# Forgetting attention with the values as TensorE's loaded operand, and its output normalised by channels

## The chip, the core and the metric

The kernel is one program on one NeuronCore of a Trainium2 chip. The core has five engines that run at the same time, each with its own list of instructions, which it works through in the order in which it stands: TensorE (PE in the profile) multiplies matrices, VectorE (DVE) and ScalarE (ACT) work on tiles elementwise, GpSimd (POOL) does so in software, and SyncE (SP) issues most of the transfers. An engine waits at an instruction until what the instruction reads has been written and the buffer that it writes is free; what stands behind it in the list waits too. The metric is the device time of one execution in microseconds (us).

## The reference, cut to what matters

Two layers work on a sequence of 256 tokens with 2048 channels. Each layer has three token mixers side by side, an output projection, and a feed-forward network. The change is in the first mixer, attention with a forget gate ("fox"): 8 heads of 64 channels.

```python
c = jnp.cumsum(jax.nn.log_sigmoid(f_logit + f_bias), axis=1)
for i in range(S // 128):                       # two blocks of 128 queries
    s = einsum('bhqd,bhkd->bhqk', q[q0:end], k[:end]) * scale
    s = s + c[q0:end, None] - c[None, :end]
    p = softmax(where(mask, s, -inf), axis=-1)
    outs.append(einsum('bhqk,bhkd->bhqd', p, v[:end]))
...
fox = rmsnorm(fox, fox_out_norm[l])             # over the 512 channels of a token
mix = concatenate([fox, gla, lru], axis=-1) @ w_out[l]
x = x + mix
```

## The kernel before, in words

Every large product is made of float32 numbers that are split in two parts, high and low. A weight block is loaded (`raw`), ScalarE casts it to the high part `wh`, VectorE subtracts to get the low part `wl`, and TensorE adds three products (hi by `wh`, hi by `wl`, lo by `wh`). The left side of a product is held transposed, channels on partitions, also as hi and lo.

The output projection is two such products, `op` 0 and 1, each of 1024 output columns and 16 steps k of 128 channels. One step is 12 matmuls of 512 columns: two token blocks, two column halves, three products. `wh` and `wl` have four buffers each, so ScalarE and VectorE can be at most four steps ahead of TensorE. The steps go through the mixers' outputs in the order `mt[2]`, `mt[3]` (the recurrent branch), `mt[1]` (gated linear attention), `mt[0]` (fox): fox's channels are steps 12 to 15 of 16, and the last two steps run after a regrouping (lines L207 to L209 instead of L216 to L219).

The softmax of fox is woven into the first of the two products: the generator `softmax` is resumed once a step. Its work goes by units: unit 0 and 1 hold four heads each of the first query block (h = 0, 128 keys), units 2 to 5 two heads each of the second (h = 1, 256 keys). They are taken in three pairs. For a pair TensorE makes the scores (`fs`), VectorE adds the gate bias and takes the row maximum, ScalarE takes the exponential and sums it by rows (`pt`, `sums`), TensorE transposes the weights (`pp`, line L938) and ScalarE copies them out (`pT`). `attend(h)` then multiplies: `pT` is loaded into the array (128 keys by 128 queries) and 64 channels of values are streamed, so that the output `fo` has queries on partitions. It is divided by the sums (L953), squared and summed (L957), and multiplied by 1/sqrt(mean square), which GpSimd computes as a power of -0.5 of one number per partition (`rstd_of`, L172). At the end `split_T` transposes the result (`tp`, L181), multiplies by the gain and writes hi and lo into `mt[0]`. The other norms of the kernel use `rstd_of` too, with one to four numbers per partition.

The program is written in the order of the data; a scheduler then sets the order of each engine's list from priorities (casts and subtractions of weights come first) and from its own estimate of durations. The small PSUM tiles (`auxt`) share two buffers.

Of the kernel before, what the change touches and what calls it, by code (L numbers as in the profile page):

```python
# [9 lines left out]
F32 = mybir.dt.float32  # L10
# [6 lines left out]
P = 128  # L17
L = 2
S = 256
NH = 2  # L20
# [28 lines left out]
def trunk(ctx, tc, x, xcols, w_in, w_out, w_gate, w_up, w_down, vecs, w2, wblk, gfin, consts, masks, out):  # L49
# [66 lines left out]
        nc.sync.dma_start(mflat, masks.rearrange("p a b -> p (a b)"))  # L116
        V.tensor_copy(msk.rearrange("p a b -> p (a b)"), mflat)

    mhalf = cp.tile([P, 8], F32, name="mhalf")
    V.memset(mhalf, -0.5)  # L120

    ls4 = cp.tile([P, L, NCT], F32, name="ls4")
# [356 lines left out]
    def mixers(l, xt, steps, mp):  # L479
# [413 lines left out]
            with tc.high_priority(SOONEST):  # L893
                V.tensor_tensor(fk[:, i], fk[:, i], bx, op=ALU.mult)
        rest(steps)
        sums = mp.tile([P, NH, 8], F32, name="sums", tag="sums")
        pTs, ons = {}, []
        units = [(h, [2 * b + e for b in range(b0, b0 + 4 // (h + 1))])
                 for h in range(NH) for b0 in range(0, 4, 4 // (h + 1)) for e in range(2)]

# [10 lines left out]
        def weights_of(n, sp):  # L911
            h, hds = units[n]
            nk, per = P * (h + 1), len(hds)
            pt = mp.tile([P, per, nk], F32, name="pt", tag=("gqk0", "gqk1", "la")[n % 3])
            mx = sm.tile([P, 4], F32, name="mx", tag="mx")
            for i, hd in enumerate(hds):
                if h == 0:
                    V.tensor_tensor_reduce(pt[:, i, :], sp[:, i * nk:(i + 1) * nk], nb00[:, hd, :], 1.0, -3.0e38,
                                           ALU.subtract, ALU.max, mx[:, i:i + 1])
                else:  # L920
                    for kb in range(2):
                        sl = slice(kb * P, (kb + 1) * P)
                        V.tensor_tensor_reduce(pt[:, i, sl], sp[:, i * nk + kb * P:i * nk + (kb + 1) * P], ck[kb][:, hd, :], 1.0,
                                               -3.0e38, ALU.subtract, ALU.max, mx[:, 2 * kb + i:2 * kb + i + 1])
# [1 line left out]
                V.tensor_tensor(mx[:, 0:2], mx[:, 0:2], mx[:, 2:4], op=ALU.max)  # L926
            V.tensor_scalar(mx[:, :per], mx[:, :per], -1.0, None, op0=ALU.mult)
            for i, hd in enumerate(hds):
                A.activation(pt[:, i, :], pt[:, i, :], AF.Exp, bias=mx[:, i:i + 1], accum_out=sums[:, h, hd:hd + 1])
            return pt  # L930

        def flip(n, pt):
# [8 lines left out]
            for i, hd in enumerate(hds):  # L941
                pTs[h, hd] = pT[:, i, :]

        def attend(h):
            o = auxt("fo")
            for hd in range(FOX_H):
                sl = slice(hd * 64, (hd + 1) * 64)
                for kb in range(h + 1):
                    T.matmul(o[:, sl], pTs[h, hd][:, kb * P:(kb + 1) * P], fv[kb][:, sl], start=kb == 0, stop=kb == h)
            rs = sm.tile([P, 8], F32, name="rs", tag="rs")  # L950
            V.reciprocal(rs, sums[:, h, :])
            on = mp.tile([P, FOX_W], F32, name="on", tag="gz", bufs=2)
            V.tensor_tensor(on.rearrange("p (h d) -> p h d", d=64), o.rearrange("p (h d) -> p h d", d=64),  # L953
                            rs.unsqueeze(2).to_broadcast([P, 8, 64]), op=ALU.mult)
            fss = sm.tile([P, 1], F32, name="fss", tag="fss")
            jk = mp.tile([P, FOX_W], F32, name="jk", tag="b1")
            A.activation(jk, on, AF.Square, accum_out=fss)  # L957
            rf = rstd_of(fss, FOX_W, 1, f"rf{l}{h}")
            V.tensor_scalar(on, on, rf, None, op0=ALU.mult)
            ons.append(on)  # L960

        mt[0] = mp.tile([P, 2, 4, S], F32R, name="mt0", tag="tok")

        def softmax():
            for n in range(0, len(units), 2):
                pts = pair(n)
                yield
                if n == 2:
                    attend(0)
                yield  # L970
                for e in range(2):
                    flip(n + e, pts[e])
                yield
            attend(1)
            yield
            for j in (0, 2):
                yield
                split_T(lambda h, i: ons[h][:, i * P:(i + 1) * P], lambda i: vc(V_FOXN + i), mt[0], j, 2)


        order = [2, 3, 1, 0]
# [89 lines left out]
```

## Time and profile before

| what | us |
|---|---|
| median of three runs | 2075.72 |
| lowest and highest run | 2075.49, 3631.46 |
| the profiled execution | 2075.76 |
| its span, first to last instruction | 2074.0 |

The profiled execution is one of those whose time agrees with the median; the 3631.46 us run is not what the profile shows. Between the span and the execution's time lie 1.8 us. A view of the profile names an engine, a source line, the operation, and the tiles it writes and reads (out<-in). A float32 matmul stands there as two rows, so that the 8 matmuls of `attend(0)` are 16 rows. TensorE's rows overlap: a matmul's own duration is longer than the distance to the next one, and it is the distance that counts.

### The profile page before, as it was taken

What the parts mean: (1) busy time and instruction counts of PE and PEld (TensorE: products, weight loads), DVE (VectorE), ACT (ScalarE), POOL (GpSimd) and SP (SyncE); (2) the same over time, 40 slices, a digit from 0 to 9 for tenths busy, and PEclk for the clock granted to TensorE, in tenths of its full rate; (3) what the DMA queues carried; (4) which work ended last, traced back from release to release, by engine and by line L of the source; (5) the groups of instructions that cost most, each with busy time, mean ns of one, the idle gap of its engine ahead of it and who ended that gap; (6) DMA issues with size and microseconds to landing.
All of it is one profiled execution on the core that took longest, in us unless ns stands there. A gap on an engine that the chain in (4) does not pass through costs nothing.

```text
span 2074.0 us, 30220 instructions
## 1 busy us (share of the span) xinstructions
PE 2058.0 (99%) x11918; PEld 1860.4 (90%) x11918; DVE 1333.5 (64%) x1730; ACT 1109.1 (53%) x1557; POOL 15.6 (1%) x26
## 2 busy tenths in 40 slices
PE   9999999999999999999999999999999999999998
PEld 7899888999998899998899998899999888999987
DVE  7787755666655556655578878666666555665654
ACT  6875555545543445554468655555555444455543
POOL 0000000000000000000000000000000000000000
PEclk9999999999999999999999999999999999999999
DMA  8566545666666666666655665456666666666664
GB/s 320 159 195 194 186 160 186 200 203 203 204 203 200 206 203 200 198 199 202 198 193 173 187 217 163 161 191 203 203 203 199 198 204 206 199 199 200 201 203 163
DMA packets 302878, 408.76 MB, mean 197 GB/s; under 512 B 11744, under 2 KB 196624, under 8 KB 302608
## 3 DMA queue, kind: packets, MB, share of 16 engines
q1 hardware_dynamic: 298112, 403.14, 59.9%
q10 hardware_dynamic: 4624, 3.70, 0.6%
q8 instruction: 93, 1.52, 0.3%
q14 instruction: 49, 0.40, 0.1%
HBM read 404.68 MB, written 2.11 MB: 196 GB/s over the span
## 4 chain that ended last, share of the span: by engine, by line
PE 96%; issue 2%; DVE 1%; ACT 0%; POOL 0%; ACTq 0%; POOLq 0%
PE gu L263 30%; PE gu L264 15%; PE dn L219 6%; PE dn L217 6%; PE dn L216 6%; PE lg L263 2%; PE op L216 2%; PE op L219 2%; PE op L217 2%; PE lx L263 2%; PE dn L208 1%; PE dn L209 1%; PE dn L207 1%; PE gqk L263 1%; PE fq L263 1%
## 5 line engine op out<-in xcount | busy, mean ns | idle before, releaser
L263 PE MATMUL gu<-x,wh 128*128 128x512 f32 x2816 | 914.4, 382 | 0.0
L289 DVE TENSOR_TENSOR wl<-raw,wh 128x1024 fp32r<-128x1024 f32 (+1 forms) x465 | 567.1, 1222 | 375.0 <-ACT wh L288 375.0
L264 PE MATMUL gu<-x,wl 128*128 128x256 f32 x2816 | 739.3, 273 | 0.0
L288 ACT CAST wh<-raw 128x1024 fp32r<-128x1024 f32 (+1 forms) x465 | 487.0, 1050 | 450.9 <-PE gu L263 361.2
L263 PEld LDWEIGHTS gu<-x,wh 128*128 128x128 f32 x2816 | 519.7, 189 | 64.7
L264 PEld LDWEIGHTS gu<-x,wl 128*128 128x128 f32 x2816 | 539.9, 192 | 9.3
L234 DVE TENSOR_TENSOR wl<-raw,wh 128x1024 fp32r<-128x1024 f32 (+2 forms) x288 | 351.5, 1226 | 268.1 <-ACT wh L233 267.6
L233 ACT CAST wh<-raw 128x1024 fp32r<-128x1024 f32 (+2 forms) x288 | 299.8, 1047 | 340.2 <-PE dn L219 191.5
L216 PE MATMUL dn<-wh,ht 128*128 128x512 f32 x568 | 215.6, 380 | 0.0
L217 PE MATMUL dn<-wl,ht 128*128 128x512 f32 x568 | 215.3, 379 | 0.0
L219 PE MATMUL dn<-wh,ht 128*128 128x512 f32 x568 | 169.0, 379 | 0.0
L219 PEld LDWEIGHTS dn<-wh,ht 128*128 128x128 f32 x568 | 107.4, 189 | 15.2
L217 PEld LDWEIGHTS dn<-wl,ht 128*128 128x128 f32 x568 | 107.4, 189 | 15.1
L216 PEld LDWEIGHTS dn<-wh,ht 128*128 128x128 f32 x568 | 107.4, 189 | 15.2
L314 ACT COPY half<-gu 128x256 f32<-128x256 f32 x176 | 64.9, 369 | 46.6 <-PE gu L263 40.9
L263 PE MATMUL lg<-xt,wh 128*128 128x512 f32 x256 | 86.5, 392 | 0.7 <-DVE lg L315 0.7
L263 PE MATMUL lx<-xt,wh 128*128 128x512 f32 x256 | 84.2, 388 | 2.1 <-ACT wh L288 1.9
L216 PE MATMUL op<-wh,mt 128*128 128x512 f32 x192 | 74.8, 390 | 0.0
L217 PE MATMUL op<-wl,mt 128*128 128x512 f32 x192 | 73.8, 384 | 0.0
L264 PE MATMUL lg<-xt,wl 128*128 128x256 f32 x256 | 67.2, 273 | 0.0
L264 PE MATMUL lx<-xt,wl 128*128 128x256 f32 x256 | 65.0, 275 | 0.4 <-DVE wl L289 0.2
L219 PE MATMUL op<-wh,mt 128*128 128x512 f32 x192 | 58.2, 382 | 0.0
(304 smaller groups left out, 2449.6 us busy)
## 6 DMA issues: line engine op xcount, KB each, us to landing
raw<-in_w_gate SPq DMA_DIRECT2D x176, 512.0 KB, 3.5
raw<-in_w_up SPq DMA_DIRECT2D x176, 512.0 KB, 4.5
raw<-in_w_down SPq DMA_DIRECT2D x176, 512.0 KB, 4.3
raw<-in_w_in SPq DMA_DIRECT2D x55, 1024.0 KB, 5.1
raw<-in_w_out SPq DMA_DIRECT2D x64, 512.0 KB, 4.4
raw<-in_w_in SPq DMA_DIRECT2D x17, 512.0 KB, 3.7
raw<-in_w_in SPq DMA_DIRECT2D x16, 528.0 KB, 3.7
raw<-in_w_in SPq DMA_DIRECT2D x16, 520.0 KB, 3.7
```

The lines of the kernel that those rows point to most:

```text
L207: T.matmul(out, hi, turns(wh[:, cols[i]]), start=k == 0, stop=False)
L208: T.matmul(out, hi, turns(wl[:, cols[i]]), start=False, stop=False)
L216: T.matmul(out, hi, turns(wh[:, c]), start=k == 0, stop=False)
L217: T.matmul(out, hi, turns(wl[:, c]), start=False, stop=False)
L219: T.matmul(inturn(ps[i][h][:, :segs[i][1]]), lo, turns(wh[:, c]), start=False, stop=k == nk - 1)
L233: A.copy(wh, raw[:, j:j + jn, :tot])
L234: V.tensor_tensor(wl, raw[:, j:j + jn, :tot], f(wh), op=ALU.subtract)
L263: both = lambda: T.matmul(ps[i].rearrange("p (a t u) -> p a t u", a=2, u=2), wh[:, c], turns(xk), start=k == 0, stop=k == KT - 1)
L264: low = lambda: T.matmul(inturn(ps[i][:, 0:S]), wl[:, c], turns(xk[:, 0]), start=False, stop=False)
L288: A.copy(wh[:, js], raw[:, rs, :])
L289: V.tensor_tensor(wl[:, js], raw[:, rs, :], f(wh[:, js]), op=ALU.subtract)
L314: mark(A.copy(two(c), halves_of(ps[:, S:])))
```

## The change

`weights_of` keeps the row sums of a unit (`sm4`), takes their reciprocal on VectorE and multiplies the whole weight tile `pt` (128x512) by it, before the transposes. `attend` loads 64 channels of the values and streams the 128 queries of `pT`; the output has channels on partitions, an even head in partitions 0 to 63 and an odd one in 64 to 127. ScalarE copies it to `on` and squares it; VectorE adds the four channel groups of the squares in two steps. A new function `norm` adds over partitions with a matmul against ones, which leaves the sum of squares of a query in every partition, and computes the power of -0.5 of the 128x128 tile on GpSimd; `mhalf` is made 128 wide for that. The gain, the factor and the split into hi and lo follow. The 16 transposes of `on` over both layers go away. `softmax` calls `norm(0)` one pair later than `attend(0)`, and `norm(1)` one step after `attend(1)`.

```diff
-    mhalf = cp.tile([P, 8], F32, name="mhalf")
+    mhalf = cp.tile([P, P], F32, name="mhalf")
...
             for i, hd in enumerate(hds):
-                A.activation(pt[:, i, :], pt[:, i, :], AF.Exp, bias=mx[:, i:i + 1], accum_out=sums[:, h, hd:hd + 1])
+                A.activation(pt[:, i, :], pt[:, i, :], AF.Exp, bias=mx[:, i:i + 1], accum_out=sm4[:, i:i + 1])
+            V.reciprocal(sm4[:, :per], sm4[:, :per])
+            V.tensor_tensor(pt, pt, sm4[:, :per].unsqueeze(2).to_broadcast([P, per, nk]), op=ALU.mult)
...
         def attend(h):
             o = auxt("fo")
-            for hd in range(FOX_H):
-                sl = slice(hd * 64, (hd + 1) * 64)
+            for b in range(FOX_H // 2):
                 for kb in range(h + 1):
-                    T.matmul(o[:, sl], pTs[h, hd][:, kb * P:(kb + 1) * P], fv[kb][:, sl], start=kb == 0, stop=kb == h)
-            rs = sm.tile([P, 8], F32, name="rs", tag="rs")
-            V.reciprocal(rs, sums[:, h, :])
...
-            A.activation(jk, on, AF.Square, accum_out=fss)
-            rf = rstd_of(fss, FOX_W, 1, f"rf{l}{h}")
-            V.tensor_scalar(on, on, rf, None, op0=ALU.mult)
+                    for e in range(2):
+                        hd = 2 * b + e
+                        T.matmul(o[e * 64:(e + 1) * 64, b * P:(b + 1) * P], fv[kb][:, hd * 64:(hd + 1) * 64],
+                                 pTs[h, hd][:, kb * P:(kb + 1) * P], start=kb == 0, stop=kb == h)
+            on = mp.tile([P, 4, P], F32, name="on", tag="gz", bufs=2)
+            A.copy(on, o.rearrange("p (b q) -> p b q", b=4))
+            jk = mp.tile([P, 4, P], F32, name="jk", tag="b1")
+            A.activation(jk, on, AF.Square)
+            for w in (2, 1):
+                V.tensor_tensor(jk[:, 0:w], jk[:, 0:w], jk[:, w:2 * w], op=ALU.add)
+            return on, jk
+        def norm(h, on, jk):
+            sq = auxt("bc")
+            T.matmul(sq[:, 0:P], ones, jk[:, 0], start=True, stop=True)
+            m, r = (mp.tile([P, P], F32, name=n, tag=n) for n in ("rfm", "rfr"))
+            V.tensor_scalar(m, sq[:, 0:P], 1.0 / FOX_W, EPS, op0=ALU.mult, op1=ALU.add)
+            G.tensor_tensor(r, m, mhalf, op=ALU.pow)
+            V.tensor_tensor(on, on, vec[:, l, V_FOXN:V_FOXN + 4].unsqueeze(2).to_broadcast([P, 4, P]), op=ALU.mult)
+            V.tensor_tensor(on, on, r.unsqueeze(1).to_broadcast([P, 4, P]), op=ALU.mult)
+            hi, lo = (mt[0][:, i, :, h * P:(h + 1) * P] for i in range(2))
+            A.copy(hi, on)
+            V.tensor_tensor(lo, on, f(hi), op=ALU.subtract)
...
-            for j in (0, 2):
-                yield
-                split_T(lambda h, i: ons[h][:, i * P:(i + 1) * P], lambda i: vc(V_FOXN + i), mt[0], j, 2)
+            last = attend(1)
+            yield
+            norm(1, *last)
+            yield
```

In the changed kernel's line numbers, L906 is the scores, L940 the transposes `pp`, L955 `fo`, L968 the matmul against ones (its output tile is called `bc`), L970 and L971 the mean square and the power, L972 and L973 the gain and the factor, L975 and L976 hi and lo.

Where the instructions stand is shown at the two norms of the first layer; the second layer's lists are the same there. First VectorE's list of the kernel before, around the norm of query block 0; `rf` is GpSimd's power of one column, `wl` (L234) are low weight parts:

```order
L953 TENSOR_TENSOR on<-fo,rs 128x512 [waits PE_49]
L926 TENSOR_TENSOR mx<-mx 128x2 [waits DVE_49]
L927 TENSOR_SCALAR mx<-mx 128x2 [waits DVE_49]
L170 TENSOR_SCALAR rf00m<-fss 128x1 [waits Activation_49]
L959 TENSOR_SCALAR on<-on,rf_2787 128x512 [waits Pool_49]
L234 TENSOR_TENSOR wl<-raw,wh 128x1024 [waits DMAHW5_49,DMAHW4_49,Activation_49]
```

The same place in the changed kernel; the first `wl` here is step 10 of the first product, the first `pt` is unit 4, the second unit 5:

```order
L970 TENSOR_SCALAR rfm<-bc 128x128 [waits PE_49]
L930 RECIPROCAL sm_2852<-sm_2852 128x2 [waits Activation_49]
L931 TENSOR_TENSOR pt<-pt,sm_2852 128x512 [waits DVE_49]
L973 TENSOR_TENSOR on<-on,rfr 128x512 [waits Pool_49]
L234 TENSOR_TENSOR wl<-raw,wh 128x1024 [waits DMAHW7_49,DMAHW6_49,Activation_49]
L930 RECIPROCAL sm_2865<-sm_2865 128x2 [waits Activation_49]
L976 TENSOR_TENSOR mt_2617<-on,mt_2617 128x4x128 [waits Activation_49]
L931 TENSOR_TENSOR pt<-pt,sm_2865 128x512 [waits DVE_49]
L234 TENSOR_TENSOR wl<-raw,wh 128x1024 [waits Activation_49]
```

Before, the wait for GpSimd stands ahead of one multiplication and the weights' low parts; now it also stands ahead of the multiplication of unit 5's softmax weights.

TensorE's list of the changed kernel, from the last row of step 7 on; the `bc` of query block 0, the matmul against ones, stands 12 matmuls earlier, ahead of step 7. The first four `pp` are unit 4, the last row is unit 5's first:

```order
L219 MATMUL op_0_1_1_2663<-wh,mt_109 128x512
L940 MATMUL pp<-cst,pt 128x128 [waits DVE_49,PE_49,Activation_49]
L940 MATMUL pp<-cst,pt 128x128
L940 MATMUL pp<-cst,pt 128x128 [waits Activation_49]
L940 MATMUL pp<-cst,pt 128x128
L216 MATMUL op_0_0_0_2660<-wh,mt_2401 128x512
L217 MATMUL op_0_0_0_2660<-wl,mt_2401 128x512
L216 MATMUL op_0_1_0_2662<-wh,mt_2401 128x512
L217 MATMUL op_0_1_0_2662<-wl,mt_2401 128x512
L219 MATMUL op_0_0_0_2660<-wh,mt_2401 128x512
L940 MATMUL pp<-cst,pt 128x128 [waits DVE_49,Activation_49]
```

The same transposes in TensorE's list before, between steps 7 and 8:

```order
L219 MATMUL op_0_1_1_2658<-wh,mt_109 128x512
L938 MATMUL pp<-cst,pt 128x128 [waits PE_49,Activation_49]
L938 MATMUL pp<-cst,pt 128x128
L938 MATMUL pp<-cst,pt 128x128 [waits Activation_49]
L938 MATMUL pp<-cst,pt 128x128
L938 MATMUL pp<-cst,pt 128x128 [waits PE_49,Activation_49]
```

They waited for ScalarE's exponentials; now they wait for VectorE as well, and unit 5's have moved five matmuls into step 8.

The norm of query block 1, in VectorE's list before:

```order
L953 TENSOR_TENSOR on<-fo,rs 128x512 [waits DVE_49,PE_49]
L170 TENSOR_SCALAR rf01m<-fss 128x1 [waits Activation_49]
L959 TENSOR_SCALAR on<-on,rf_2959 128x512 [waits Pool_49]
L234 TENSOR_TENSOR wl<-raw,wh 128x1024 [waits Activation_49]
L234 TENSOR_TENSOR wl<-raw,wh 128x1024 [waits DMAHW3_49,DMAHW2_49,Activation_49]
```

and in the changed kernel, where the one `wl` between L973 and L976 is step 13:

```order
L962 TENSOR_TENSOR jk<-jk 128x256 [waits Activation_49]
L972 TENSOR_TENSOR on<-on,vec 128x512
L962 TENSOR_TENSOR jk<-jk 128x128 [waits DVE_49]
L970 TENSOR_SCALAR rfm<-bc 128x128 [waits PE_49]
L973 TENSOR_TENSOR on<-on,rfr 128x512 [waits Pool_49]
L234 TENSOR_TENSOR wl<-raw,wh 128x1024 [waits Activation_49]
L976 TENSOR_TENSOR mt_2617<-on,mt_2617 128x4x128 [waits Activation_49]
```

TensorE's list of the changed kernel has the second `bc` after step 9, then steps 10 and 11, and then step 12, the first that reads fox's `mt[0]` (here `mt_2617`); its first six matmuls are of query block 0, the others of block 1:

```order
L219 MATMUL op_0_0_0_2660<-wh,mt_2617 128x512
L219 MATMUL op_0_1_0_2662<-wh,mt_2617 128x512
L216 MATMUL op_0_0_1_2661<-wh,mt_2617 128x512 [waits Activation_49]
L217 MATMUL op_0_0_1_2661<-wl,mt_2617 128x512
L216 MATMUL op_0_1_1_2663<-wh,mt_2617 128x512
L217 MATMUL op_0_1_1_2663<-wl,mt_2617 128x512
L219 MATMUL op_0_0_1_2661<-wh,mt_2617 128x512 [waits DVE_49]
```

In the kernel before, two groups of four transposes `tp` stood there, one after step 10 and one after step 11; now nothing but the steps stands between the second `bc` and the wait.

## Rows read from the trace of the kernel before

**Rows 1.** The page: busy time, share of span, instructions; chain that ended last, by engine.

```profile
PE 2058.0 (99%) x11918; PEld 1860.4 (90%) x11918; DVE 1333.5 (64%) x1730; ACT 1109.1 (53%) x1557; POOL 15.6 (1%) x26
...
PE 96%; issue 2%; DVE 1%; ACT 0%; POOL 0%; ACTq 0%; POOLq 0%
```

**Rows 2.** TensorE's waits in the whole span: total us, times, longest.

```profile
PE lx L263 <- ACT wh L288: 1.9, 2, 1.4
```

**Rows 3.** Windows of the first layer's softmax stretch: busy us of each engine, clock, DMA.

```profile
255.00:265.00 10.00, 10.00 (x58) 7.67 (x57) 6.68 (x25) 7.77 (x25) 0.00 (x0) 1.00 0.34 107
265.00:275.00 10.00, 10.00 (x54) 8.16 (x54) 6.03 (x27) 5.82 (x14) 0.55 (x1) 1.00 0.41 125
```

**Rows 4.** GpSimd's groups by shape: busy us, mean ns of one, idle before.

```profile
L717 POOL MEMSET kt<- 128x512 f32 x4 | 2.0, 524 | 689.4 <-PE dn L209 689.1 <-POOLq L1060 0.3
L702 POOL MEMSET gqm<- 128x1024 f32 x2 | 1.9, 960 | 147.0 <-DVE ti L565 147.0
L172 POOL TENSOR_TENSOR r<-r400m,mhalf 128x4 f32<-128x4 f32 x1 | 1.0, 1008 | 44.8 <-DVE r400m L170 44.8
...
L172 POOL TENSOR_TENSOR r<-r21m,mhalf 128x2 f32<-128x2 f32 x1 | 0.7, 701 | 63.4 <-DVE r21m L170 63.4
...
L172 POOL TENSOR_TENSOR rf<-rf00m,mhalf 128x1 f32<-128x1 f32 x1 | 0.5, 547 | 42.4 <-DVE rf00m L170 42.4
```

**Rows 5.** Timeline of the first norm: start, duration, engine, line, idle before and releaser.

```profile
266.56 0.55 POOL L172 TENSOR_TENSOR rf<-rf00m,mhalf 128x1 f32<-128x1 f32 x1 [42.43 <-DVE rf00m L170]
267.15 0.49 DVE L959 TENSOR_SCALAR on<-on,rf 128x512 f32<-128x512 f32 x1 [0.66 <-POOL rf L172]
```

**Rows 6.** VectorE's groups by shape, 245 to 303 us.

```profile
L234 DVE TENSOR_TENSOR wl<-raw,wh 128x1024 fp32r<-128x1024 f32 x16 | 19.5, 1224 | 13.2 <-ACT wh L233 12.9
...
L953 DVE TENSOR_TENSOR on<-fo,rs 128x512 f32<-128x512 f32 x2 | 1.4, 690 | 1.2 <-PE fo L949 1.2
...
L951 DVE RECIPROCAL rs<-sums 128x8 f32<-128x8 f32 x2 | 0.4, 198 | 0.0
...
L170 DVE TENSOR_SCALAR rf00m<-fss 128x1 f32<-128x1 f32 x1 | 0.2, 154 | 0.5 <-ACT jk L957 0.5
```

**Rows 7.** ScalarE's groups by shape, 245 to 303 us.

```profile
L940 ACT COPY pT<-pp 128x512 f32<-128x512 f32 x6 | 3.3, 574 | 0.1
...
L957 ACT ACTIVATE jk<-on 128x512 f32<-128x512 f32 x2 | 1.3, 634 | 4.3 <-DVE on L953 4.3
```

**Rows 8.** TensorE's timeline, first layer's output projection.

```profile
250.60 1.88 PE L907 MATMUL fs<-fk,fq 64*128 64x128 f32 x16 [0.73 <-DVE mt L186]
252.42 0.48 PE L209 MATMUL op<-wh,mt 128*128 128x512 f32 x1
...
276.48 1.09 PE L938 MATMUL pp<-cst,pt 128*128 128x128 f32 x8
277.32 0.46 PE L216 MATMUL op<-wh,mt 128*128 128x512 f32 x1
...
279.99 3.68 PE L949 MATMUL fo<-fv,pT 128*128 128x64 f32 x32
283.48 0.46 PE L216 MATMUL op<-wh,mt 128*128 128x512 f32 x1
...
286.15 0.38 PE L216 MATMUL op<-wh,mt 128*128 128x512 f32 x1
...
288.74 0.60 PE L181 MATMUL tp<-cst,on 128*128 128x128 f32 x4
289.10 0.46 PE L216 MATMUL op<-wh,mt 128*128 128x512 f32 x1
```

**Rows 9.** Windows at the end of the span: columns as in rows 3.

```profile
2064.00:2066.00 2.00, 1.36 (x7) 0.85 (x5) 1.72 (x3) 0.95 (x3) 0.00 (x0) 1.00 0.85 314
...
2068.00:2070.00 2.00, 0.00 (x0) 0.00 (x0) 0.88 (x2) 1.33 (x2) 0.03 (x1) 0.50 0.28 109
```

**Rows 10.** TensorE's timeline at the start of the span.

```profile
1.19 4.45 PE L104 MATMUL wp<-warm 128*128 128x512 bf16 x10 [1.19 <-DVE xp L523]
```

More of the change, by code (lines that the diff above doesn't have):

```diff
@@ L895, in mixers @@
         rest(steps)
-        sums = mp.tile([P, NH, 8], F32, name="sums", tag="sums")
-        pTs, ons = {}, []
+        pTs = {}
         units = [(h, [2 * b + e for b in range(b0, b0 + 4 // (h + 1))])
@@ L915, in weights_of @@
             mx = sm.tile([P, 4], F32, name="mx", tag="mx")
+            sm4 = sm.tile([P, 4], F32, name="sm4", tag="sm4")
             for i, hd in enumerate(hds):
@@ L942, in flip @@
                 pTs[h, hd] = pT[:, i, :]
+        mt[0] = mp.tile([P, 2, 4, S], F32R, name="mt0", tag="tok")
         def attend(h):
             o = auxt("fo")
-            for hd in range(FOX_H):
-                sl = slice(hd * 64, (hd + 1) * 64)
+            for b in range(FOX_H // 2):
                 for kb in range(h + 1):
-                    T.matmul(o[:, sl], pTs[h, hd][:, kb * P:(kb + 1) * P], fv[kb][:, sl], start=kb == 0, stop=kb == h)
-            rs = sm.tile([P, 8], F32, name="rs", tag="rs")
@@ L951, in attend @@
-            V.reciprocal(rs, sums[:, h, :])
[L952 to L956, printed above, removed]
-            A.activation(jk, on, AF.Square, accum_out=fss)
-            rf = rstd_of(fss, FOX_W, 1, f"rf{l}{h}")
@@ L959, in attend @@
-            V.tensor_scalar(on, on, rf, None, op0=ALU.mult)
-            ons.append(on)
-        mt[0] = mp.tile([P, 2, 4, S], F32R, name="mt0", tag="tok")
+                    for e in range(2):
[3 more added lines that the diff above has]
+            on = mp.tile([P, 4, P], F32, name="on", tag="gz", bufs=2)
@@ L964, in softmax @@
         def softmax():
+            last = None
             for n in range(0, len(units), 2):
@@ L968, in softmax @@
                 if n == 2:
-                    attend(0)
+                    last = attend(0)
+                elif n == 4:
+                    norm(0, *last)
                 yield
@@ L973, in softmax @@
                 yield
-            attend(1)
+            last = attend(1)
             yield
-            for j in (0, 2):
-                yield
-                split_T(lambda h, i: ons[h][:, i * P:(i + 1) * P], lambda i: vc(V_FOXN + i), mt[0], j, 2)
+            norm(1, *last)
+            yield
         order = [2, 3, 1, 0]
```

## The prediction

> **What bounds the kernel now.** I read the page's busy times first, then the chain of work that ended last, then TensorE's waits. TensorE is busy 99% of the span and makes up 96% of the chain [rows 1], and its longest sum of waits for one thing is 1.9 us [rows 2]. So every microsecond that is added to or taken from TensorE's list counts, and so does every wait that the change puts into it, while work on the other engines costs something only where TensorE comes to wait for it. Then I read the windows of the stretch that the change touches: in the softmax stretch of the first layer TensorE has no idle time at all, VectorE is busy 6.0 to 6.7 us in 10 and ScalarE 5.8 to 7.8 [rows 3]. There is room for some more work there, but each of these engines goes through its list in order, so what matters is where in the list a long wait stands.
>
> **The power on GpSimd.** This is the term that decides. Before, GpSimd raises one, two or four numbers per partition: 547 ns, 701 ns and 1008 ns [rows 4]. One more column costs 154 ns, two more 307 ns, so the time is 0.394 + 0.1535 us for each column, on a straight line through all three sizes. The change raises 128 columns: 0.394 + 128 x 0.1535 = **20.0 us** for one, and there are four (two query blocks, two layers). The line is carried 32 times beyond its last point. As a bound from below, the memsets show what GpSimd needs for a column when the arithmetic is nothing: (960 - 524) / 512 = 0.85 ns [rows 4], which would make the power 0.4 + 0.1 = 0.5 us. I take the line, because three shapes of the very same operation lie on it to within a few ns and the memset is another operation. The Trainium skill (GPSIMD Engine Reference, section 3.1, Elementwise) gives about 2.6 cycles for an element of a two-input elementwise operation at 1.2 GHz, which would be 0.3 us for 128 columns plus the fixed part; no row here shows a power at that rate, and the rows have some 70 times as much per column. What it would make of the time is the first rival.
>
> **The first wait, query block 0.** Before, GpSimd's 0.55 us cost VectorE 0.66 us of idle time [rows 5], and TensorE nothing. Now VectorE stands at the multiplication L973 for the whole power. Behind it in its list stand the low weights of step 10, the low part of fox's block 0, and the multiplication of unit 5's softmax weights, and TensorE's transposes of unit 5 wait for that last one. The four weight buffers don't help, since TensorE stops at the transposes in the middle of step 8. From the start of the power to the transposes it takes 20.0 + 0.69 (L973, by L953's 128x512) + 1.22 (`wl`) + 0.20 (reciprocal) + 0.69 (low part) + 0.69 (unit 5) = 23.5 us [rows 6]; ScalarE's cast of the high part, 0.57 us [rows 7], lies beside the `wl`. What TensorE still has after `bc`: step 7, 12 matmuls or 2.59 us (286.15 to 288.74), four transposes at 0.84 / 8 = 0.105 us each, and five matmuls at 0.216 us, in all 4.1 us [rows 8]. Between `bc` and the start of the power lie a handing over and the mean square of 0.15 us [rows 5, 6], at least 0.4 us, and up to 1.5 us if VectorE is still at unit 4 and 5's maxima; I take 0.6. So the stall is 23.5 + 0.6 - 4.1 = **20.0 us**, in both layers.
>
> **The second wait, query block 1.** From the second `bc` it is 0.4 + 20.0 + 0.69 (L973) + 0.57 (the cast L975, by L940's copy) + 0.1 = 21.8 us until ScalarE has written the high part [rows 6, 7]. TensorE's cover is steps 10 and 11 and the first half of step 12: 2 x 2.59 + 6 x 0.216 = 6.5 us [rows 8]. The low part comes after a `wl`, 1.22 + 0.69 us after L973, and TensorE has four matmuls (0.86 us) before it needs that: 0.3 us more. The stall is 21.8 - 6.5 + 0.3 = **15.6 us**. The chain from `fo` to `bc` (copy 0.57, square 0.63, additions and gain) is covered by step 9 except for a few tenths, which I leave out. Both waits together: 35.6 us a layer, 71.2 us in all.
>
> **The clock after the waits.** At the end of the span TensorE's last work lies in the window 2064 to 2066 us, at a granted clock of 1.00; in the window 2068 to 2070 us, with nothing to do, it is 0.50 [rows 9], that is 1.2 GHz in place of 2.4. At the start of the span, where it comes out of idleness, ten matmuls of 512 columns take 4.45 us, 0.445 us each [rows 10], against 0.216 us later. Each of the four waits is longer than the idle time at the end of the span, so TensorE comes back at half clock: at most 10 x (0.445 - 0.216) = 2.3 us lost for each, at least 0 where it would wait anyway. I take 2.0, as the stretches that follow are dense: **8 us**.
>
> **What TensorE gains and pays.** The 16 transposes of `on` go: four take 0.36 us (288.74 to 289.10), so -1.4 us. Four matmuls against ones come, each two rows; the rows of `fo` are the nearest at 3.49 / 32 = 0.109 us: +0.9 us. The 96 rows of `fo` change shape [rows 8]: before, 128 columns are loaded and 64 streamed, 0.109 us a row; after, 64 are loaded and 128 streamed. If even and odd heads run in the two halves of the array's columns at the same time, a row can come down to 128 / 512 x 0.216 = 0.054 us, -5.3 us; if not, the scores of 128 columns, 1.82 / 16 = 0.114 us a row, give +0.5 us. I take -2.5 us, between them, as neither row has 64 loaded columns. The Trainium skill (TensorE: Matmul & The Clock Gate, Part 3, Packing small matmuls) says that matmuls with outputs at different partition groups run concurrently, which would be the first end; the trace before shows no such matmul.
>
> **The other engines.** VectorE gets per layer six reciprocals and six multiplications of 128x512 (0.20 + 0.69 each) ahead of the transposes, and loses the work on `on` [rows 6]. In the first two pairs of units, the transposes come up to 2 x 0.89 us later per pair than ScalarE's exponentials alone would allow. TensorE's list has steps to do meanwhile; uncovered it would be at most 4 x 1.78 = 7.1 us over both layers, at least 0. I take 2 us. The third pair's is in the first wait already. The wider `mhalf` is one memset at the start and costs nothing beside the first loads. The casts and copies that ScalarE gets and loses are about even, and its queue holds no long wait ahead of the weights.
>
> **The sum.** 71.2 + 8 - 1.4 + 0.9 - 2.5 + 2 = +78 us on the profiled execution's 2075.76 us, which is the median of the runs to 0.04 us: **2154 us**, 3.8% more. Bounds of this case: hand-overs 4 us shorter, no loss by the clock, `fo` at its best and no waits for transposes give 2075.8 + 67.2 - 1.4 + 0.9 - 5.3 = 2137; hand-overs 2 us longer, 9.2 for the clock, `fo` at 0.5 and 7.1 for the transposes give 2166.
>
> **Rivals.**
> - *The power is cheap.* GpSimd runs over 128 columns at the memset's pace, 0.5 us. Then the first wait is 0.5 + 3.5 + 0.6 - 4.1 = 0.5 us and the second is covered (2.3 us against 6.5): 2075.8 + 1.0 - 1.4 + 0.9 - 2.5 + 2 = 2076 us, no change. Here the sign is decided: 2% are 41.5 us, and since both waits of both layers grow by 4 us for each us of the power, the change is slower by that only if the power takes more than about 11 us. For it: I extrapolate from small shapes, where a fixed pipeline might weigh. Against it: such a cost would bend the line between one, two and four columns, and it doesn't bend. Chance 0.09.
> - *The power is dear, but in larger tiles at half the cost a column*, 10 us: the first wait is 10, the second 5.6 us, and the clock costs some 6: 2075.8 + 31.2 + 6 - 1 = 2112 us, 1.7% more, within the 2%. For it: a loop could take two columns at a time once it has them; against it: four columns show no sign of it. Chance 0.06.
> - *TensorE stays at half clock between the two waits*, 12 to 15 matmuls and 16 rows of `fo` longer than taken, or GpSimd is slowed by other engines while VectorE works on: 5 us more for each layer and more, 2164 to 2180 us. Chance 0.05.
> - *The column halves don't overlap.* This changes 3 us and no sign, and is in the range.
>
> **How the numbers follow.** The forecast has 0.80, and most of it lies in 2137 to 2166; the half-cost rival's 2112 and the cheap one's 2076 stay out. The range 2130 to 2170 leaves out about 0.2. Slower by over 2% (what a measurement here can tell from no change; above 2117.2 us): the forecast and the dear rival, 0.85. Within 2%: 0.14. Faster: 0.01, since TensorE's list itself gives back 3 us at the most likely and some 6 us at best, 0.3%.
>
> **What would show it.** In the changed kernel's profile, four powers L971 of about 20 us each; VectorE idle before L973 by nearly as much, released by GpSimd; TensorE waiting twice a layer, once in the transposes L940 of unit 5 released by VectorE, once at step 12 released by ScalarE's cast; a granted clock of 0.5 in windows behind these; `fo` at 0.05 to 0.11 us a row; and no new waits anywhere else. If the powers are short, the whole forecast falls. If they are 20 us long and the time is still near 2076, then the lists stand differently from what I read.

## The result, and the profile after

| | us |
|---|---|
| after, median of four runs | 2156.53 (2155.25 to 2157.12) |
| before, median beside it | 2075.64 |
| the profiled execution of after | 2155.25, its span 2153.5 |

The time is 1.0389 times that of before (95% interval 1.0377 to 1.0401): 81 us, 3.9% slower. One of the four runs of before took 3631.46 us, and the ratio leaves it out. Spans are compared below, 2153.5 against 2074.0 us, 79.5 us more.

The page of the changed kernel, busy times and the chain that ended last, against [rows 1]:

```profile
PE 2062.9 (96%) x11910; PEld 1860.3 (86%) x11910; DVE 1343.9 (62%) x1754; ACT 1110.4 (52%) x1553; POOL 96.5 (4%) x26
...
PE 91%; POOL 4%; issue 2%; DVE 2%; ACT 1%; POOLq 0%; ACTq 0%
```

TensorE is busy 4.9 us longer, and a slower clock (below) is part of that; the other 74.6 us of the difference are time in which it stands. GpSimd, which had no share in the chain before, now has 4% of it, some 80 us. GpSimd's groups by shape show which instruction that is; [rows 4] has the old one, of 547 ns:

```profile
L971 POOL TENSOR_TENSOR rfr<-rfm,mhalf 128x128 f32<-128x128 f32 x4 | 83.1, 20778 | 128.2 <-DVE rfm L970 128.2
```

TensorE's waits in the whole span (engine, tile and line, releaser, total us, times, longest), where [rows 2] had 1.9 us as the largest:

```profile
PE pp L940 <- DVE pt L931: 41.4, 2, 20.7
PE op L216 <- ACT mt L975: 32.4, 2, 16.2
```

Two places, each once a layer, make 73.8 of the 79.5 us. Neither names GpSimd: the view says who released TensorE last, and between GpSimd and TensorE stand VectorE and ScalarE. The chain, followed in order of time through the first layer's first wait (start, us, what), shows them:

```profile
274.79 0.17 DVE mx L927
274.96 0.20 DVE rfm L970
...
275.23 20.79 POOL rfr L971
...
296.65 1.22 DVE wl L234
297.87 0.07 DVE sm L930
297.94 0.48 DVE mt L976
...
298.45 0.69 DVE pt L931
...
299.28 1.08 PE pp L940 x4
```

This is VectorE's list as it stood in the section on the change: after the multiplication by GpSimd's result (L973) a low weight part, a reciprocal, the low part of fox's block 0, and then the softmax weights of unit 5, for which TensorE's transposes wait. Only the last of them needs to be there for TensorE; the others, and GpSimd's 20.8 us ahead of them, are in its way because VectorE takes its list in order.

Windows of the two waits (columns as in [rows 3], which has TensorE busy throughout the 20 us ahead of this place):

```profile
275.00:285.00 10.00, 3.57 (x19) 2.80 (x17) 1.04 (x3) 2.20 (x7) 9.77 (x1) 0.90 0.24 86
285.00:295.00 10.00, 0.00 (x0) 0.00 (x0) 0.00 (x0) 0.00 (x0) 10.00 (x1) 0.50 0.00 0
...
315.00:325.00 10.00, 0.01 (x1) 0.00 (x0) 0.00 (x0) 0.00 (x0) 10.00 (x1) 0.61 0.00 0
```

For ten whole microseconds GpSimd is the only thing on the core that moves. Even the transfers stop, which fits that the weight buffers come free only when TensorE goes on. The granted clock falls to 0.50, and TensorE's timeline behind the two waits shows what that costs:

```profile
299.28 1.08 PE L940 MATMUL pp<-cst,pt 128*128 128x128 f32 x4 [20.71 <-DVE pt L931]
...
300.58 0.63 PE L216 MATMUL op<-wh,mt 128*128 128x512 f32 x1
301.01 0.63 PE L217 MATMUL op<-wl,mt 128*128 128x512 f32 x1
...
331.21 0.79 PE L216 MATMUL op<-wh,mt 128*128 128x512 f32 x1 [16.20 <-ACT mt L975]
331.80 0.63 PE L217 MATMUL op<-wl,mt 128*128 128x512 f32 x1
...
334.33 0.38 PE L217 MATMUL op<-wl,mt 128*128 128x512 f32 x1
```

Matmuls of 512 columns follow each other by 0.43 us, twice the 0.216 us of before. From 299.28 to 303.28 us that loses some 2 us, from 331.21 to 334.33 us some 1.5 us. In the second layer more is lost. There the clock is still at half when `fo` of the second query block runs, as TensorE's timeline and two windows show:

```profile
1366.37 1.08 PE L940 MATMUL pp<-cst,pt 128*128 128x128 f32 x4 [20.71 <-DVE pt L931]
...
1370.37 2.71 PE L955 MATMUL fo<-pT,fv 128*64 128x128 f32 x32
1373.01 0.48 PE L216 MATMUL op<-wh,mt 128*128 128x512 f32 x1
```

```profile
1370.00:1371.00 1.00, 1.00 (x8) 0.63 (x8) 0.00 (x0) 0.52 (x1) 0.00 (x0) 0.50 0.97 315
1372.00:1373.00 1.00, 1.00 (x20) 0.84 (x16) 0.78 (x1) 0.00 (x0) 0.00 (x0) 1.00 0.35 135
```

`fo` takes 2.64 us there, where the first layer has 2.02 us (303.28 to 305.30), and behind the second wait, from 1398.92 to 1402.79 us, some 1.8 us are lost.

### The profile page after: what moved, and what is told of

It reads as the page before. It is cut to its first block, busy times and chain, and to the rows that moved or that the text cites. A ratio compares the mean times of both kernels' runs of the same rounds, so it can differ in the third digit from the quotient of the medians.

```text
span 2153.5 us, 30215 instructions
## 1 busy us (share of the span) xinstructions
PE 2062.9 (96%) x11910; PEld 1860.3 (86%) x11910; DVE 1343.9 (62%) x1754; ACT 1110.4 (52%) x1553; POOL 96.5 (4%) x26
## 3 DMA queue, kind: packets, MB, share of 16 engines
q8 instruction: 93, 1.52, 0.3%
## 4 chain that ended last, share of the span: by engine, by line
PE 91%; POOL 4%; issue 2%; DVE 2%; ACT 1%; POOLq 0%; ACTq 0%
PE gu L263 29%; PE gu L264 14%; PE dn L217 6%; PE dn L219 6%; PE dn L216 6%; POOL rfr L971 4%; PE lg L263 2%; PE lx L263 2%; PE op L216 2%; PE op L219 2%; PE op L217 2%; PE gqk L263 1%; PE fq L263 1%; PE dn L208 1%; PE dn L207 1%
## 5 line engine op out<-in xcount | busy, mean ns | idle before, releaser
L234 DVE TENSOR_TENSOR wl<-raw,wh 128x1024 fp32r<-128x1024 f32 (+2 forms) x288 | 351.1, 1225 | 261.1 <-ACT wh L233 260.7
L216 PE MATMUL op<-wh,mt 128*128 128x512 f32 x192 | 77.6, 404 | 32.4 <-ACT mt L975 32.4
L971 POOL TENSOR_TENSOR rfr<-rfm,mhalf 128x128 f32<-128x128 f32 x4 | 83.1, 20778 | 128.2 <-DVE rfm L970 128.2
L216 PEld LDWEIGHTS op<-wh,mt 128*128 128x128 f32 x192 | 37.8, 197 | 39.4 <-ACT mt L975 33.2
```

The source lines that it names most:

```text
L216: T.matmul(out, hi, turns(wh[:, c]), start=k == 0, stop=False)
L234: V.tensor_tensor(wl, raw[:, j:j + jn, :tot], f(wh), op=ALU.subtract)
L971: G.tensor_tensor(r, m, mhalf, op=ALU.pow)
```

## The experiments

Each kernel is timed beside the kernel before, whose median was 2075.68 us in the first seven and 2075.60 us in the last three.

**Half the power.** The changed kernel; GpSimd raises 64 of the 128 columns; the others are set to 1, so the kernel leaves the norm's factor out for half of the queries.

```diff
-            G.tensor_tensor(r, m, mhalf, op=ALU.pow)
+            G.memset(r[:, 64:], 1.0)
+            G.tensor_tensor(r[:, :64], m[:, :64], mhalf[:, :64], op=ALU.pow)
```

> The changed kernel, but GpSimd raises only the first 64 of the 128 columns; the other 64 are set to 1, so that the norm's factor is left out for half of the queries. If the length of the power is what costs (the theory), it takes about 10.6 us in place of 20.8, both waits of both layers shrink by 10.2 us, to about 10.5 and 6, and the time is 2156.5 - 41 = 2116 us, a little less if the shorter waits cost less clock. If the power only stands where the time is lost, and the added work on VectorE or the new order of the lists holds TensorE (the rival), the time stays near 2156 us.

Measured: 2114.49 us (2113.82 to 2115.22), 1.0187 times before (1.0173 to 1.0201). GpSimd's group of this kernel, and below it TensorE's waits:

```profile
L972 POOL TENSOR_TENSOR rfr<-rfm,mhalf 128x64 f32<-128x64 f32 x4 | 42.2, 10549 | 124.7 <-DVE rfm L970 124.7
```

```profile
PE pp L940 <- ACT mt L976: 20.4, 2, 10.2
PE op L216 <- ACT mt L976: 11.8, 2, 5.9
```

The power is 10.23 us shorter, and each wait is shorter by that to within 0.3 us (20.7 to 10.2, 16.2 to 5.9). The time falls by 42.0 us, 4 x 10.23 = 40.9 and 1 us more.

**Four columns of power.** The same with 4 in place of 64.

> The changed kernel, but GpSimd raises only 4 of the 128 columns and the rest are set to 1 (the norm's factor is left out for 124 of 128 queries). Theory: the power takes 1.0 us as in the kernel before, the second wait is covered, the first is 1 us or less, the clock stays up, and what is left is the rest of the change: 2156.5 - 73.8 (four waits) - 7.5 (clock) + 2 x 0.9, about 2076 us, 2072 to 2079. Rival (the other work of the change costs something of its own): clearly above 2080 us.

Measured: 2075.77 us (2075.63 to 2075.91), 1.0000 times before (0.9992 to 1.0009). GpSimd needs 1008 ns, and the waits are these:

```profile
PE pp L940 <- DVE pt L931: 1.4, 2, 0.7
PE pp L940 <- ACT mt L976: 1.3, 2, 0.7
```

So the whole of the 81 us goes with the length of the power. It also leaves a question: the work that TensorE is spared (below) should have made this kernel faster than before, and it is not. Its rows, added from the start of one to the start of the next, say where that went. In a layer `fo` takes 2.27 us less than before, and the transposes that are gone, less the matmuls against ones, 0.36 us. Against these 2.6 us stand 1.35 us in the two waits above, 0.43 us in the scores of the second pair of units (1.80 us for 1.37) and 0.44 us in the transposes `pp` (2.47 us for 2.03), together 2.2 us.

**A later consumer.** The powers are as in the changed kernel, but the factor, the cast and the low part of block 0 stand behind block 1's mean square in VectorE's list, so that the wait for GpSimd no longer stands ahead of unit 5's weights. `norm` ends with the power now, and `scaled` holds the gain, the factor, hi and lo.

```diff
...
-            norm(1, *last)
+            second = norm(1, *last)
+            yield
+            yield
+            with tc.issue_after(second[2]):
+                scaled(0, *first[:2])
+            scaled(1, *second[:2])
```

> The changed kernel with the same four powers of 128 columns, but the multiplication by the factor of query block 0, the cast and the low part are moved in VectorE's and ScalarE's lists behind the second mean square; so no softmax weight and no weight block stands behind the first power any more. Theory: the first wait goes, but GpSimd must still do both powers one after the other, 41.6 us from the first mean square on, and step 12 waits for the second: TensorE gets to step 12 about 13 us earlier than in the changed kernel for each layer, 2156.5 - 25 = 2131 us, with one wait of some 27 us per layer. Rival (only the place in VectorE's list costs, and the power itself would be covered): both first waits go and nothing comes back, 2156.5 - 45 = 2111 us.

Measured: 2129.54 us (2129.0 to 2129.77), 1.0259 times before (1.0244 to 1.0275). TensorE's waits of this kernel, and below them GpSimd in the timeline of the first layer:

```profile
PE op L219 <- DVE mt L980: 36.7, 2, 18.4
PE op L216 <- ACT mt L979: 12.0, 2, 6.0
```

```profile
274.97 41.52 POOL L971 TENSOR_TENSOR rf<-rf,mhalf 128x128 f32<-128x128 f32 x2 [50.79 <-DVE rf L970]
```

The long wait at the transposes is gone, and 27 us of the 81 with it. The rest stays, because GpSimd has 41.5 us to do for a layer and step 12 needs both results: the powers run back to back and TensorE waits for their sum, 6.0 + 18.4 us a layer. With the steps in this order, a better place in the list cannot hide more than the steps between `bc` and step 12 last. Even here VectorE's list holds something up:

```profile
295.79 0.94 DVE L977 TENSOR_TENSOR on<-on,rf 128x512 f32<-128x512 f32 x1 [7.50 <-POOL rf L971]
316.52 0.69 DVE L977 TENSOR_TENSOR on<-on,rf 128x512 f32<-128x512 f32 x1 [19.80 <-POOL rf L971]
317.13 0.69 DVE L980 TENSOR_TENSOR mt<-on,mt 128x512 fp32r<-128x512 f32 x1
```

The 18.4 us wait is for the low part of block 0 (L980), which needs only the first power, but stands behind the multiplication by the second (L977 at 316.52). Little hangs on it: only two matmuls of block 0 read it, and what follows them needs the second power anyway.

**The long power in the kernel before.** Nothing of the change but the length of the power: `rstd_of` is replaced by a power of 128 equal columns, of which one is used.

```diff
...
-            rf = rstd_of(fss, FOX_W, 1, f"rf{l}{h}")
-            V.tensor_scalar(on, on, rf, None, op0=ALU.mult)
+            r = mp.tile([P, P], F32, name="rfm", tag="rfm")
+            V.tensor_scalar(r, fss.to_broadcast([P, P]), 1.0 / FOX_W, EPS, op0=ALU.mult, op1=ALU.add)
+            G.tensor_tensor(r, r, mhalf, op=ALU.pow)
+            V.tensor_scalar(on, on, r[:, 0:1], None, op0=ALU.mult)
```

> The kernel before, with nothing of the change but the wide power: the mean square of a query, one number per partition, is written to 128 equal columns, GpSimd raises all 128, and one of them is used. Theory: the power takes 20.8 us, VectorE stands at the multiplication after it with the low weights of steps 8 and 9 and the maxima of units 4 and 5 behind it, TensorE waits some 17.5 us at the transposes of unit 4 and 18 us at the transposes of the output, and with 2 us of clock for each wait the time is 2075.6 + 79 = 2155 us, 2148 to 2160. Rival (the wide power hurts only in the order and with the added work of the change): less than 2110 us, and 2076 us if it is covered.

Measured: 2155.28 us (2154.7 to 2155.81), 1.0384 times before (1.037 to 1.0398), as long as the whole change. TensorE's waits:

```profile
PE tp L181 <- DVE on L961: 35.8, 2, 17.9
PE pp L938 <- ACT pt L929: 33.0, 4, 15.7
```

They are at other places, since the lists are the old ones, but they add up to 68.8 us, and the mechanism is the same: at `pp` the exponentials wait for maxima that stand behind VectorE's wait for GpSimd. The values as loaded operand, the weights normalised beforehand and the output by channels are not needed for the loss.

**One column of power, spread afterwards.** The whole change, with the sum of squares formed as one number per partition (the squares are loaded, one column of ones is streamed), raised by `rstd_of`, and spread over partitions by a product of ones and a diagonal.

```diff
...
-            T.matmul(sq[:, 0:P], ones, jk[:, 0], start=True, stop=True)
...
-            G.tensor_tensor(r, m, mhalf, op=ALU.pow)
+            T.matmul(sq[:, 0:1], jk[:, 0], ones[:, 0:1], start=True, stop=True)
+            return rstd_of(sq[:, 0:1], FOX_W, 1, f"rf{l}{h}")
...
+            V.tensor_scalar(dg, ident, r, None, op0=ALU.mult)
+            T.matmul(rb[:, 0:P], ones, dg, start=True, stop=True)
...
```

> The whole change, but the sum over partitions is made with the squares as the loaded operand, so that a query's sum of squares lies in its own partition: GpSimd raises one number per partition (0.55 us as before the change), and a diagonal matrix and a matmul against ones spread it over the partitions again. Theory: with the wide power gone both waits go: 2076 us, 2073 to 2079, no change against the kernel before, no power longer than 0.6 us and no wait of TensorE over 1.5 us in the stretch. Rival (the new order of the work needs the waits whatever the power): over 2100 us.

Measured: 2074.76 us (2074.41 to 2075.08), 0.9996 times before (0.9987 to 1.0005). The change's aim can be had without its loss, but not with a gain that can be told from none.

**Even heads, then odd heads.** The kernel of the last experiment, with the eight heads of `attend` not in pairs but all even ones ahead of all odd ones.

```diff
-            for b in range(FOX_H // 2):
-                for kb in range(h + 1):
-                    for e in range(2):
+            for e in range(2):
+                for b in range(FOX_H // 2):
+                    for kb in range(h + 1):
```

> The kernel of the one-column power, with the products of the attention in another order: first all even heads, then all odd ones, so that no two neighbours lie in different halves of the array's columns. If the 0.064 us a row in place of 0.109 come from the two halves running at the same time, the rows go back to about 0.107 us and the 96 rows cost 4.1 us more than in the kernel of the one-column power, some 2080 us. If they come from loading 64 columns in place of 128 (the rival), the rows stay at 0.064 us and the time stays the same.

Measured: 2078.42 us (2078.2 to 2078.6), 1.0013 times before (1.0004 to 1.0022), and 3.7 us more than the pairs. TensorE's timeline around `fo` of the second query block, first in pairs:

```profile
281.12 1.97 PE L955 MATMUL fo<-pT,fv 128*64 128x128 f32 x32
283.01 0.48 PE L216 MATMUL op<-wh,mt 128*128 128x512 f32 x1
```

and unpaired:

```profile
281.39 3.33 PE L955 MATMUL fo<-pT,fv 128*64 128x128 f32 x32
284.65 0.48 PE L216 MATMUL op<-wh,mt 128*128 128x512 f32 x1
```

From the start of `fo` to the next matmul it is 1.89 us in pairs, 0.059 us a row, against 3.26 us, 0.102 us a row, unpaired; in the first query block 1.03 against 1.52 us for 16 rows, 0.064 and 0.095. The difference, 1.86 us a layer, is the 3.7 us. The loads have 64 columns in both, so the gain comes from neighbours in different column halves, not from smaller loads. The unpaired rows are near the 0.109 us of the old form [rows 8].

**The softmax weights normalised beforehand, alone.** The kernel before, with `weights_of` as changed, and `fo` only copied.

```diff
...
+            V.reciprocal(sm4[:, :per], sm4[:, :per])
+            V.tensor_tensor(pt, pt, sm4[:, :per].unsqueeze(2).to_broadcast([P, per, nk]), op=ALU.mult)
...
-            V.tensor_tensor(on.rearrange("p (h d) -> p h d", d=64), o.rearrange("p (h d) -> p h d", d=64),
-                            rs.unsqueeze(2).to_broadcast([P, 8, 64]), op=ALU.mult)
+            V.tensor_copy(on, o)
```

> The kernel before with one part of the change: the softmax weights are multiplied by the reciprocals on VectorE ahead of the transposes, and the output is only copied where it was divided. Theory: what the new shape of the attention gains (4.3 us) and the missing transposes (0.5 us net) was eaten in the run with the short power by this work, which makes the transposes come later: 2 to 4 us more, 2078 to 2080 us, with TensorE idle before transposes. Rival: it is covered by the steps, 2075.7 us, and the gain went elsewhere.

Measured: 2080.07 us (2079.81 to 2080.42), 1.0021 times before (1.0012 to 1.003). This is 4.4 us, as much as the pairs of heads give. It is a cost in the kernel before, and not the one that four columns of power left open: there the waits are longer and the scores lose 0.43 us a layer (above), here it is the other way round. TensorE's wait that the edit brings is short (`PE pp L940 <- DVE pt L931`, 0.9 us in all). More of it is in the scores, here of the third pair of units, in TensorE's timeline of this kernel:

```profile
270.86 1.13 PE L906 MATMUL fs<-fk,fq 64*128 64x256 f32 x4
271.91 0.48 PE L216 MATMUL op<-wh,mt 128*128 128x512 f32 x1
...
272.54 1.13 PE L906 MATMUL fs<-fk,fq 64*128 64x256 f32 x4
273.60 0.48 PE L216 MATMUL op<-wh,mt 128*128 128x512 f32 x1
```

and in that of the kernel before:

```profile
270.12 1.14 PE L907 MATMUL fs<-fk,fq 64*128 64x256 f32 x8
271.19 0.48 PE L216 MATMUL op<-wh,mt 128*128 128x512 f32 x1
```

The same eight rows of scores take 1.07 us before (270.12 to 271.19) and 1.05 + 1.06 us now; those of the second pair take 1.37 us before and 1.80 now. Heads are 64 channels, an even one in the upper half of the array's rows and an odd one in the lower. Before, the rows of the third pair start two at a time, 0.01 us apart, which fits even and odd heads by turns. Here the transposes of the two units come apart; the reading is that their score tiles come free one after the other, and that the scheduler therefore puts two matmuls of one unit ahead of two of the other. In the rows the two pairs lose 0.43 + 1.04 = 1.5 us a layer, 2.9 us in all; with the wait's 0.9 us that makes 3.8 of the 4.4 us.

**The scores held in alternating order.** This is to test that reading, in three kernels: the one-column version, the one with the weights normalised alone, and the kernel before. The first score matmul is of the unit whose tile comes free last, and each further one is tied behind the one ahead of it.

```diff
-                for _, _, hds, sp in both:
-                    T.matmul(sp[:, i * nk:(i + 1) * nk], rows(fq, hds[i], slice(h * P, (h + 1) * P)),
-                             rows(fk, hds[i], slice(0, nk)), start=True, stop=True)
+                for _, _, hds, sp in reversed(both):
+                    with contextlib.nullcontext() if prev is None else tc.issue_after(prev):
+                        prev = T.matmul(sp[:, i * nk:(i + 1) * nk], rows(fq, hds[i], slice(h * P, (h + 1) * P)),
+                                        rows(fk, hds[i], slice(0, nk)), start=True, stop=True).ins
```

> The one-column version of the whole change, with the score matmuls of a pair of units held in the order even head, odd head, even head, odd head. In the traces so far eight rows of scores of 256 keys take 1.07 us where the heads alternate, 1.80 us where two of one head stand ahead of two of the other, and 2.11 us where other matmuls stand between them. Theory (the two row halves of the array overlap only if even and odd heads alternate, and the change lost this in the second group of scores): the second group gains 1.80 - 1.07 = 0.7 us a layer, and the first, whose 16 rows of 128 keys take 1.82 us, up to 0.8 us; 2074.8 - 1.4 to 3.0 = 2071.8 to 2073.4 us, a little faster than the kernel before. Rival (a group's time is set by something else, such as the transposes beside it): 2074.8 us as without the edit.

Measured: 2077.34 us (2076.93 to 2077.78), 1.0008 times before (0.9999 to 1.0017).

> The kernel before with the softmax weights normalised ahead of the transposes, and the scores held in alternating order. Theory (most of the 4.4 us that this normalisation cost is lost in the scores, whose two later groups take 1.80 and 2.11 us in place of 1.37 and 1.07): 2080.1 - 2 x (0.7 + 1.0) and up to 1.6 more from the first group, 2075.1 to 2076.7 us. Rival (the time goes in waits for VectorE's multiplications): only the first group can gain, 2078.5 to 2080.1 us.

Measured: 2079.21 us (2079.0 to 2079.46), 1.0017 times before (1.0009 to 1.0026).

> The kernel before with the scores held in alternating order; nothing else is changed. Theory: the last group alternates already (1.07 us), the second gains 1.37 - 1.07 = 0.3 us a layer, the first, whose 16 rows take 1.82 us with three matmuls of one tile ahead of three of the other, up to 0.8 us: 2075.7 - 0.6 to 2.2 = 2073.5 to 2075.1 us. Rival (order doesn't matter): 2075.7 us.

Measured: 2076.19 us (2076.05 to 2076.3), 1.0003 times before (0.9994 to 1.0012).

The theory's numbers fail in all three. The first was to gain 1.4 to 3.0 us and lost 2.6, the second gained 0.9 where 3.4 at least were expected, the third lost 0.6 where 0.6 to 2.2 were to be gained; the second's time lies in the rival's range. TensorE's timeline of the second kernel shows the second group of scores:

```profile
263.73 0.70 PE L909 MATMUL fs<-fk,fq 64*128 64x256 f32 x2
264.36 0.48 PE L218 MATMUL op<-wl,mt 128*128 128x512 f32 x1
...
264.99 1.13 PE L909 MATMUL fs<-fk,fq 64*128 64x256 f32 x6
266.05 0.48 PE L220 MATMUL op<-wh,mt 128*128 128x512 f32 x1
```

Rows that alternate can be faster: in the first group of this kernel, of 128 keys, 14 rows take 1.08 us (251.47 to 252.55), 0.077 us a row, where [rows 8] has 16 in 1.82, 0.114 us a row. But in the first two kernels the edit let the first matmul of each group go ahead alone: two rows by themselves take 0.63 us, two long matmuls (of 512 columns) stand behind them, and the group has 0.63 + 1.06 = 1.69 us in place of 1.80. That is also a second border between scores and long matmuls, and at each border the next long matmul comes 0.3 us on and not 0.216. In the third kernel only the first group was cut so; the other two stayed whole:

```profile
260.45 1.44 PE L910 MATMUL fs<-fk,fq 64*128 64x256 f32 x8
261.82 0.48 PE L217 MATMUL op<-wh,mt 128*128 128x512 f32 x1
...
270.20 1.24 PE L910 MATMUL fs<-fk,fq 64*128 64x256 f32 x8
271.37 0.48 PE L217 MATMUL op<-wh,mt 128*128 128x512 f32 x1
```

They take 1.37 and 1.17 us, where the kernel before has 1.37 and 1.07: the second group did not gain the 0.3 us that the theory gave it. So an alternating order in a whole group does not suffice for 1.07 us, and what sets a group's time stays open. The test did not separate the theories as it was meant to. The rows of the two timelines show that most of the 4.4 us lies in the scores; that the order of the heads is the reason is argued and not shown. The versions with normalised weights were not tried with alternating groups that stay whole.

## Why the prediction was right

**The power.** 20.0 us were predicted, 20.78 measured; 64 columns take 10.55 and four take 1.008 us. From 4 to 64 and from 64 to 128 columns it is 0.159 and 0.160 us for each more, against 0.1535 from one to four. So the straight line of [rows 4] held to 128 columns with a slope 4% too small. The first rival, a cheap power, is out, and with it the figure of the Trainium skill (GPSIMD Engine Reference, section 3.1, Elementwise) as a price for this operation: its 2.6 cycles an element at 1.2 GHz stand against 0.16 us, some 190 cycles, and the measurement decides. The half-cost rival is out as well, but its price was a fair one: it gave 2112 us for a power of 10 us, and the kernel with 64 columns, with 10.55 us, takes 2114.5 us.

**The first wait.** 20.0 predicted, 20.7 measured, and the power's 0.8 us account for it. From the start of the power to the transposes the chain has 24.05 us (275.23 to 299.28) for 23.5: 0.8 us more for the power, some 0.2 us less for the steps behind it. Before the start, VectorE was still at unit 5's maxima (`mx` in the chain), and the mean square took 0.2 to 0.3 us and not 0.15, so that the power started 1.0 us behind `bc` and not 0.6; TensorE's cover, 4.35 us for 4.1, took back most of that.

**The second wait.** 15.6 predicted, 16.2 measured, again the power's 0.8. The 0.3 us for the low part did not come up: VectorE wrote it ahead of any need. Both waits: 73.8 us, 71.2 predicted.

**The clock.** 8 us predicted; read from the rows, 2 + 1.5 us in the first layer and 2 + 0.6 (in `fo`) + 1.8 us in the second, about 8 in all. It stayed at half for 3 to 6 us after each wait and was at 1.00 again ahead of the next, so the rival in which it stays at half between the waits did not happen.

**TensorE's own work.** For `fo` -2.5 us was taken between -5.3 and +0.5. In this kernel the two blocks have 1.02 us (264.23 to 265.25) and 2.02 us (303.28 to 305.30, its start at half clock) in the first layer, where before there were 1.70 and 3.49 us: -4.3 us for two layers, with the second layer's 0.6 us counted under the clock. The middle that was taken was 1.8 us short. The column halves do overlap, as the Trainium skill says of small matmuls in different column tiles (TensorE: Matmul & The Clock Gate, Part 3), and the unpaired order shows that this is the cause. The transposes' -1.4 us is their count and price as before; the matmuls against ones cost 0.7 us for 0.9.

**The other engines.** The 2 us taken for the later transposes were foreseen as waits. In this kernel TensorE waits for nothing in the first two pairs of units. What was lost there is in the scores of the second pair (1.80 us, as 261.58 to 263.38 shows, for 1.37), some 0.9 us in all, and in the transposes `pp`, some 0.8 us at full clock. So the size came out near, and not for the reason given. In the kernel before, the normalised weights alone cost 4.4 us, more than twice the term.

The sum by rows: 73.8 + 8 - 4.3 - 1.4 + 0.7 + 0.9 + 0.8 = 78.5 of 79.5 us. Of the other 1.0 us, 0.3 lie ahead of the first scores (250.92 us for 250.60); the rest is not assigned. That the total came nearer than its terms is in part luck, since errors of opposite sign met: the waits were 2.6 us longer than forecast, and `fo` 1.8 us shorter. The terms of the forecast's upper bound add up to 2165 us and not 2166, on which nothing hangs. What the errors of the terms share is that they are small beside one term: 4 us for each us of the power, which half of it (42.0 us for 40.9) and the kernel before with the long power alone (79.6 us) both confirm.

## What to carry to other kernels

Ahead of an operation on GpSimd such as this power, ask how many columns it gets: a statistic that a matmul has spread over all partitions costs it one column for each token, where one number per partition costs one column, and spreading afterwards by a matmul is far cheaper (2074.8 against 2156.5 us). Price such an operation from its own rows at several sizes, and then read in the lists of the engines what stands behind its consumer; the wait shows up at an engine and a line that have nothing to do with it. Work for TensorE that is saved can be lost again in short waits and in the order of its list: small matmuls for the two column halves must stand next to each other to overlap, and a group of small matmuls that is cut pays at each cut.

## What was not expected of the hardware

Two neighbours in the column halves take 0.059 to 0.064 us a row of 64 loaded and 128 streamed columns, against 0.095 to 0.102 us where the halves do not alternate; for row halves it is less clear (eight rows of 64 x 256: 1.07, 1.17 or 1.37 us for groups that alternate, by the rows or by the edit, and 1.80 us where two matmuls of one unit stand ahead of two of the other). Waits of 0.7 us left the granted clock at 1.00 in their windows; those of 5.9 us and more took it to half, where it stayed for 3 to 6 us after TensorE came back, or until the next wait where that came first.
